# A third of unit 3's columns on ScalarE's DMA queue, and ScalarE's share of the normalisation in units 2 and 3

## The chip, the cores and the metric

The kernel runs on one core of one Trainium2 chip. Such a core has TensorE (PE), VectorE (DVE), ScalarE (ACT) and GpSimd (POOL), a sequencer SyncE (SP) that here only issues transfers, and 16 DMA engines between HBM and the on-chip memory (SBUF, 128 partitions). The metric is the device time of one execution in microseconds (us); the median of several runs counts, and one further execution was recorded by the hardware profiler.

## The reference

The input x has the shape (4, 8, 16, 256, 256) in float32: 512 channels of 65,536 elements, 134.2 MB. Each channel is normalised by its own mean and variance and multiplied by the channel's gamma:

```python
mu = x.mean(axis=(3, 4), keepdims=True)
var = ((x - mu) ** 2).mean(axis=(3, 4), keepdims=True)
x_norm = (x - mu) / np.sqrt(var + 1e-5)
out = x_norm * gamma[None, :, :, None, None]
```

The output is as large as the input, so 268.5 MB have to cross between HBM and SBUF.

## The kernel before

**Units.** The 512 channels are cut into 22 units, numbered from 0. The first and the last hold 16 channels, the 20 between them hold 24 (line 34). A unit is stored as 128 partitions of 2 or 3 columns, where a "column" is F = 4096 elements, 16 KB per partition. So a unit of two is 4 MiB (4.19 MB), a unit of three 6 MiB (6.29 MB), and each partition's part lies in one piece in HBM. A unit of three spreads each channel over partition thirds, so its column j has its own scale and shift on each partition. Four slots of SBUF (line 56) hold the units in turn; unit u lives in slot u % 4, is normalised in place and stored from there.

**Loads.** `load(u)` (lines 61 to 66) issues one DMA on SP's queue for a unit. Where `split` has an entry for the unit, its first column or columns go on ACT's queue instead, by a DMA of their own (line 64), and SP's DMA (line 66) takes the rest. Before the change only unit 1 is split, one column of three. The loads of units 0 to 3 are issued at once at the start; the load of unit u + 4 stands in the program behind the store of unit u (line 239) and waits on SP until that store has landed, since it takes the same slot.

**One unit's work** (lines 156 to 239). DVE sums the columns (line 161, or 165 for the units of two) while ACT squares them with an accumulated sum, column by column (line 168). TensorE adds the sums over the partitions of each channel (line 179 or 183), DVE forms the negative variance (187), ACT takes the root (191), DVE the reciprocal and the product with gamma (197, 204). In the units of three, TensorE spreads the two coefficients back to the partitions, into the tile `wide` (208). Then the columns are normalised: DVE takes them one by one (line 221), three of them, or two if the unit is in `helped`; in that case two small DVE instructions (214, 215) prepare the tile `own`, and ACT normalises the third column (216). In a unit of two that is helped, ACT takes 3/8 of the columns (229) and DVE the rest (233). The unit's store is issued by ACT, on ACT's queue (237).

**What sets the order.** Every engine works through its own instructions in the order of the program, unit after unit; semaphores hold it back where it needs another engine's result or a transfer. SP's queue therefore carries nothing but loads in the order of the units, and ACT's queue carries unit 1's first column and then the stores in the order of the units. Both queues are served by the same 16 DMA engines: a DMA over 128 partitions gives each engine 8 rows (one row is the piece of one partition: 16, 32 or 48 KB) and a short write to the semaphore at the end.

The lines that the change touches are these two:

```python
    split = {1: 1}

    helped = (0, 1)
```

Of the kernel before, what the change touches and what calls it, by code (L numbers as in the profile page):

```python
# [15 lines left out]
def kernel(  # L16
# [19 lines left out]
    starts = [sum(sizes[:i]) for i in range(U)]  # L36
    assert 8 * sum(sizes) == n_ch

    split = {1: 1}

    helped = (0, 1)

    xf = x.rearrange("b g c h w -> (b g c h w)")
    of = out.rearrange("b g c h w -> (b g c h w)")
# [225 lines left out]
```

## Time and profile before

| what | value |
|---|---|
| median of three runs | 627.42 us (627.4, 627.42, 630.28) |
| the profiled execution, its own time | 626.98 us |
| its span, from the first to the last instruction | 625.1 us |
| DVE busy | 438.4 us (70%) |
| ACT busy | 251.5 us (40%) |
| PE busy | 39.1 us (6%) |
| DMA | 268.50 MB, mean 430 GB/s over the span |
| share of the DMA engines' time | 50.4% for ACT's queue (q10), 49.1% for SP's (q1) |

The busy times are sums over the span; an engine that is busy for 70% isn't the limit for that reason alone. The share of the DMA engines' time by queue adds up to 99.5%, and that is the number to keep in mind. The profile's page cuts the span into 40 slices of 15.6 us and gives for each the busy share of every engine in tenths and the rate of the DMA in GB/s. Further views used below are the chain of work that ended last (in order of time), the list of who waited for whom, the instructions of one line with the times of their DMAs from issue to landing, the timeline of one engine, and stretches of time with the busy time of each engine and the DMA rate. "Landing" is the moment when the semaphore of a DMA is complete.

### The profile page before, as it was taken

The page shows a single profiled execution, that of the slowest core. Times are in us where ns is not written, and L with a number is a line of the kernel's source. Part 1 is how long each engine was busy: PE and PEld are TensorE (multiplying, and loading weights), DVE is VectorE, ACT ScalarE, POOL GpSimd, SP SyncE. Part 2 cuts the span into 40 slices and gives each one's busy share as a digit, 9 for nine tenths or more (in the row PEclk, how much of TensorE's full clock was granted, in tenths as well). Part 3 has the DMA queues.
Part 4 walks back from the last instruction along what each step waited for, and adds up shares of the span by engine and source line. Part 5 has one row for each costly group of instructions (what it writes and reads, how often), then busy time and mean ns, then how long its engine had stood idle before and what let it go on. Part 6 is the DMA issues. An engine that isn't in the chain of part 4 may idle for free.

```text
span 625.1 us, 1082 instructions
## 1 busy us (share of the span) xinstructions
PE 39.1 (6%) x280; PEld 36.6 (6%) x280; DVE 438.4 (70%) x179; ACT 251.5 (40%) x150; POOL 4.4 (1%) x17
## 2 busy tenths in 40 slices
PE   1000110101010100101010101010010101010100
PEld 1000110101010100101010101010010101010100
DVE  0789886858667585868686866758586868686780
ACT  0678253342607070615334261707062533426130
POOL 2000000000000000000000000000000000000000
DMA  9999999999999999999999999999999999999997
GB/s 384 438 400 437 437 450 406 453 431 425 450 413 440 440 421 443 434 428 443 415 447 440 418 447 428 434 440 418 443 440 421 443 425 435 443 421 426 440 441 338
DMA packets 6549, 268.50 MB, mean 430 GB/s; under 512 B 768, under 2 KB 784, under 8 KB 784
## 3 DMA queue, kind: packets, MB, share of 16 engines
q10 hardware_dynamic: 3312, 136.32, 50.4%
q1 hardware_dynamic: 3168, 132.12, 49.1%
q8 instruction: 2, 0.03, 0.0%
q14 instruction: 3, 0.02, 0.0%
q0 software_dynamic: 64, 0.01, 0.0%
HBM read 134.22 MB, written 134.23 MB: 429 GB/s over the span
## 4 chain that ended last, share of the span: by engine, by line
DMA 72%; DVE 22%; PE 1%; issue 1%; ACT 0%; SPq 0%; ACTq 0%
DMA xt<-in_x_dram 51%; DMA out_dram<-xt 22%; DVE st L161 15%; DVE xt L221 3%; DVE st L165 3%; DVE xt L233 1%; PE wide L208 1%; ACT std L191 0%; PE ps L179 0%; DVE nvar L187 0%; DVE rstd L197 0%; DVE coef L204 0%; PE ps L183 0%; DVE own L214 0%; DVE own L215 0%
## 5 line engine op out<-in xcount | busy, mean ns | idle before, releaser
L168 ACT ACTIVATE junk<-xt 128x4096 uint8<-128x4096 f32 (+1 forms) x62 | 231.0, 3727 | 290.7 <-DMA xt<-in_x_dram 278.4
L161 DVE TENSOR_REDUCE st<-xt 128x3 f32<-128x12288 f32 x20 | 259.1, 12953 | 99.5 <-DMA xt<-in_x_dram 99.5
L221 DVE TENSOR_SCALAR xt<-xt,wide 128x4096 f32<-128x4096 f32 x59 | 139.5, 2421 | 30.2 <-PE wide L208 30.2
L179 PE MATMUL ps<-st,navg 128*24 128x2 f32 x120 | 7.4, 178 | 498.7 <-DVE st L161 498.7
L179 PEld LDWEIGHTS ps<-st,navg 128*24 128x24 f32 x120 | 6.3, 126 | 499.8 <-issue 499.8
L208 PE MATMUL wide<-coef,spread 24*128 24x2 f32 x120 | 28.2, 347 | 23.0 <-DVE coef L204 23.0
L191 ACT ACTIVATE std<-nvar,eps_t 24x1 f32<-24x1 f32 (+1 forms) x22 | 6.5, 294 | 56.1 <-DVE nvar L187 56.1
L208 PEld LDWEIGHTS wide<-coef,spread 24*128 24x128 f32 x120 | 27.0, 321 | 24.1 <-issue 23.0
L165 DVE TENSOR_REDUCE st<-xt 128x1 f32<-128x8192 f32 x2 | 17.4, 8686 | 3.4 <-DMA xt<-in_x_dram 3.4
L187 DVE TENSOR_SCALAR nvar<-ps 24x1 f32<-24x1 f32 (+1 forms) x22 | 6.1, 276 | 12.6 <-PE ps L179 11.1
L168 ACT ACTIVATION_READ_ACCUMULATOR junk<-xt 128x1 f32 x62 | 11.6, 186 | 0.0
L119 DVE COPY g_two<-g_row 1x128 f32<-1x128 f32 x1 | 0.2, 214 | 11.3 <-DMA g_row<-in_gamma_dram 11.3
L197 DVE RECIPROCAL rstd<-std 24x1 f32<-24x1 f32 (+1 forms) x22 | 3.3, 152 | 6.7 <-ACT std L191 6.7
L233 DVE TENSOR_SCALAR xt<-xt,ps,coef 128x5120 f32<-128x5120 f32 (+1 forms) x2 | 7.5, 3748 | 0.0
L216 ACT ACTIVATE xt<-xt,own 128x4096 f32<-128x4096 f32 x1 | 3.8, 3803 | 2.4 <-DVE own L215 2.4
L204 DVE TENSOR_TENSOR coef<-rstd,g_col 24x1 f32<-24x1 f32 (+1 forms) x22 | 3.3, 148 | 0.8
L229 ACT ACTIVATE xt<-xt,shift,coef 128x3072 f32<-128x3072 f32 x1 | 2.9, 2947 | 0.7 <-DVE shift L228 0.7
L183 PE MATMUL ps<-st,navg 128*128 128x2 f32 x4 | 1.1, 349 | 28.4 <-DVE st L165 28.4
L196 DVE COPY coef<-ps 24x1 f32<-24x1 f32 x20 | 2.7, 135 | 0.0
L183 PEld LDWEIGHTS ps<-st,navg 128*128 128x128 f32 x4 | 1.0, 311 | 28.5 <-issue 28.5
L129 PE MATMUL g_ps<-one,g_rep 1*128 1x1 f32 x4 | 1.0, 345 | 13.0 <-DVE g_rep L126 13.0
L115 ACT ACT_TABLE_LOAD x1 | 1.3, 1283 | 1.2 <-PEq L254 1.2
(29 smaller groups left out, 10.2 us busy)
## 6 DMA issues: line engine op xcount, KB each, us to landing
out_dram<-xt ACTq DMA_DIRECT2D x20, 6144.0 KB, 49.2
xt<-in_x_dram SPq DMA_DIRECT2D x19, 6144.0 KB, 43.6
xt<-in_x_dram SPq DMA_DIRECT2D x3, 4096.0 KB, 26.3
out_dram<-xt ACTq DMA_DIRECT2D x2, 4096.0 KB, 22.1
xt<-in_x_dram ACTq DMA_DIRECT2D x1, 2048.0 KB, 17.2
out_dram<-touch POOLq DMA_DIRECT2D x1, 8.0 KB, 7.4
g_row<-in_gamma_dram POOLq DMA_DIRECT2D x1, 0.5 KB, 10.4
```

Source lines behind the costliest of these rows:

```text
L161: nc.vector.reduce_sum(out=st[:, u, :, 0], in_=t.rearrange("p (j f) -> p j f", j=3), axis=AX.X,)
L165: nc.vector.reduce_sum(out=st[:, u, 0, 0:1], in_=t, axis=AX.X)
L168: square = nc.scalar.activation(out=junk[:, :step], in_=t[:, j * step : (j + 1) * step], func=ACTF.Square, accum_out=st[:, u, j, 1:2],)
L179: nc.tensor.matmul(out=ps[:n], lhsT=navg3[:, j], rhs=st[:, u, j], start=j == 0, stop=j == 2,)
L187: nc.vector.tensor_scalar(out=nvar[:n, u : u + 1], in0=ps[:n, 0:1], scalar1=ps[:n, 0:1], scalar2=ps[:n, 1:2], op0=ALU.mult, op1=ALU.add,)
L191: nc.scalar.activation(out=std[:n, u : u + 1], in_=nvar[:n, u : u + 1], func=ACTF.Sqrt, bias=eps_t[:n], scale=-1.0,)
L197: nc.vector.reciprocal(out=rstd[:n, u : u + 1], in_=std[:n, u : u + 1])
L204: nc.vector.tensor_mul(out=coef[:n, u, 1:2], in0=rstd[:n, u : u + 1], in1=gamma_u)
L208: nc.tensor.matmul(out=wide[:, j], lhsT=spread[:, j], rhs=coef[:n, u], start=True, stop=True,)
L216: nc.scalar.activation(out=t[:, 2 * F :], in_=t[:, 2 * F :], func=ACTF.Identity, bias=own[:, 0:1], scale=own[:, 1:2],)
L221: nc.vector.tensor_scalar(out=t[:, j * F : (j + 1) * F], in0=t[:, j * F : (j + 1) * F], scalar1=wide[:, j, 0:1], scalar2=wide[:, j, 1:2], ...
L233: nc.vector.tensor_scalar(out=t[:, :cut], in0=t[:, :cut], scalar1=ps[:, 0:1], scalar2=coef[:, u, 1:2], op0=ALU.add, op1=ALU.mult,)
```

## The change

```diff
-    split = {1: 1}
-
-    helped = (0, 1)
+    split = {1: 1, 3: 1}
+
+    helped = (0, 1, 2, 3)
```

The first column of unit 3 (2.10 MB) is now loaded by a second DMA on ACT's queue, issued right behind that of unit 1 and ahead of every store; SP's DMA for unit 3 shrinks from three columns to two. In units 2 and 3 DVE normalises two columns instead of three, ACT normalises the third, and DVE runs the two small instructions for `own`. No byte more or less is moved. The order of the instructions is otherwise the same: ACT gets one DMA and two activations of 128x4096 more, DVE two tensor_scalar instructions of 128x4096 fewer and four small ones more.

## The prediction

> **What bounds the kernel now.** I read the 40 slices first, then the shares of the queues.
>
> ```profile
> span 625.1 us, 1082 instructions
> DMA  9999999999999999999999999999999999999997
> GB/s 384 438 400 437 437 450 406 453 431 425 450 413 440 440 421 443 434 428 443 415 447 440 418 447 428 434 440 418 443 440 421 443 425 435 443 421 426 440 441 338
> q10 hardware_dynamic: 3312, 136.32, 50.4%
> q1 hardware_dynamic: 3168, 132.12, 49.1%
> ```
>
> The DMA engines are busy in every slice, 99.5% over the span. The rates jitter because a transfer is counted in the slice where it starts; long stretches don't jitter, whichever queues are at work:
>
> ```profile
> 4.00:18.00 14.00, 2.35 (x36) 2.27 (x36) 1.02 (x7) 0.13 (x1) 1.74 (x5) 1.00 1.01 434
> 31.00:38.00 7.00, 0.00 (x0) 0.00 (x0) 7.00 (x2) 6.54 (x4) 0.00 (x0) 1.00 1.03 405
> 216.00:448.00 232.00, 14.23 (x96) 13.32 (x96) 165.44 (x64) 91.37 (x56) 0.00 (x0) 1.00 1.00 434
> ```
>
> The last column is GB/s: 434 for pure loads at the start, 434 for loads beside stores. 268.5 MB at 434 GB/s are 618.7 us of 625.1. The rest is the start (first data at 1.8 us), the end, and a dip at 31 to 38 us. So a change can gain almost nothing unless it moves fewer bytes, and this one moves the same. It can lose where the DMA engines run out of work. The place to look is the end, in the chain:
>
> ```profile
> 554.02 38.63 DMA xt<-in_x_dram
> 592.65 0.02 issue
> 592.67 8.70 DVE st L165
> ...
> 603.15 4.55 DVE xt L233
> ```
>
> and the waits and the stores' landing times:
>
> ```profile
> DVE st L161 <- DMA xt<-in_x_dram: 99.5, 17, 6.4
> SPq L66 <- DMA out_dram<-xt: 529.4, 18, 41.7
> DMA to landing us min/median/max: 16.3/49.2/49.8
> ```
>
> DVE waits for loads in 17 units, and SP waits for stores. The last load lands at 592.65; 15.1 us later (607.73) the last store is issued, and it lands 16.3 us after that (the minimum in the third row), at 624.05. It is 4.19 MB, 9.7 us at 434 GB/s. The fixed cost of a DMA on idle engines is read from the start: units 0 and 1a (I call unit 1's first column 1a and the rest 1b, likewise 3a and 3b), 6.29 MB, are issued at 0.81 and unit 0 lands 17.04 us later (the chain), 14.5 of them data: 2.5 us. So the last store could have landed 12.2 us after its issue; for the other 4.1 us it stood behind unit 20's store. **The last load has 4.1 us of slack; beyond that, each us that it comes later lengthens the kernel by one.**
>
> **How the queues share.** Two numbers fix it. 0 on SP's queue (32 KB rows) and 1a on ACT's (16 KB rows) land together, 17.0 and 17.2 us after their issue, and have 4 and 2 MiB: the queues take turns row by row, so shares go by row size. In steady state both have 48 KB rows and a load of 6.29 MB takes 29.0 us (ACT's first squares of units 19 and 20 start at 539.53 and 568.52), 217 GB/s, half. The last load, 32 KB rows beside 48 KB ones, takes 592.67 - 568.52 = 24.1 us: 174 GB/s, 0.4 of 434. Row by row fits all three.
>
> The Trainium skill, page "DMA: Bandwidth & Descriptors", section "Queues, rings and completion order", states that an engine round-robins between queues but drains a whole packet, typically 9 to 17 descriptors, before it switches. With the 9 of each DMA here, unit 0 would have landed about 5 us ahead of 1a; the trace has 0.2 us, so the rows speak against it. I keep it as a rival.
>
> **The change part by part.**
>
> *The DMA of 3a.* One more issue on ACT at about 1.2 us, 0.4 us long like the present one; ACT then has nothing to do until unit 0 lands at 17.87. Cost nothing. SP's issue for unit 3 stays, smaller. On ACT's queue 3a stands ahead of store 0.
>
> *18 to 32.5 us.* Up to 18 nothing changes. Then 1b had all of the bandwidth and landed at 27.5 (1.23 + 26.3). Now 1b (32 KB rows) shares 2:1 with 3a (16 KB): 6.29 MB, 14.5 us, both end at about 32.4. DVE reached unit 1 at 31.27, after normalising unit 0, so unit 1 starts 1.1 us later, and store 1 is issued at 53.6 instead of 52.44.
>
> *32.5 to 58 us.* Store 0 is issued at 31.58 as before. Its first row moved only at 36.5, by the trace's record of single transfers, which also shows that the rows under way then took 2.5 us instead of 1.8: that is the 405 GB/s above, some 0.7 us lost. Now ACT's queue was active until 32.4, and store 0 should begin at about 34 to 35. It took 23.1 us from first row to landing (59.57), so it lands at 57.8, 1.8 earlier. Unit 2 shares with it 0.6 to 0.4 from 34 on instead of running alone from 27.5: it lands at about 55.5 instead of 47.6. DVE had started unit 2 at 52.27, so it now waits 3 us for it.
>
> *58 to 83 us.* Store 1 ran beside unit 3's 48 KB rows at half rate, 29.0 us. 3b has 32 KB rows, so store 1 gets 0.6, 6.29 MB at 260 GB/s = 24.2 us, a little more once 3b is through: it lands at about 82.6 instead of 88.53, **5.9 earlier**. 3b lands at about 79 instead of 74.1.
>
> *Steady state.* From here both queues halve the bandwidth as before. The bytes moved up to any time are the same, but for at most 0.28 MB from the 0.7 us saved, so stores 5.9 us early mean loads 4.6 to 5.9 us late: I take 5.3. A load is issued when the store four units earlier lands, and had 14.5 us of lead (unit 20's row: 554.02 issue of unit 21, 568.52 its turn); that grows. Stores had lead too: issued 562.73 (unit 19), in turn at 579.6; it shrinks by about 11 us to some 6, against 2.4 at least that store 0 needed from issue to first row. No queue runs dry, so the lag stays.
>
> *The end.* The last load lands at 598.0, the last store is issued at 613.0 and lands at 613.0 + 2.5 + 9.7 = 625.2 instead of 624.05: **+1.2 us**.
>
> The Trainium skill, same page, section "Anatomy of one DMA", puts the fixed cost of a DMA at about 2.0 us; by that the loss would be 0.7. The trace's 2.5 us decides.
>
> *The help in units 2 and 3.* Each saves one of three DVE passes (7.09 to 4.75 us, the rows of units 2 and 1 at line 221) and adds two small ones (0.3 us): 2.0 us, and ACT adds 3.80 us beside DVE. Stores 2 and 3 are issued 2.0 us earlier than they otherwise would be (about 76.7 for store 2), but ACT's queue is with store 1 until 82: covered. Without that cover it would be a gain of 2.0 us per unit, at the start only. Worth: nothing. ACT's own next work, unit 3's and 4's squares, waits for loads anyway (it waited 14 us for unit 4).
>
> *Unknown: how soon a store starts when ACT's queue is nearly empty.* Nothing before shows this at the end. Nearest rows: 2.5 us fixed at the start, and store 0's 4.9 us from issue to first row (5.3 with the landing) in the middle of busy loads. I take 2.5, as the engines are idle then; the other end gives +4.0. Below, with a lag of 4.6 and 1.9 us, the slack covers all: 0.
>
> Sum: span 625.1 + 1.2 = 626.3, plus 1.9 us around it (626.98 - 625.1) = 628.2 for the profiled execution; the median of the runs stands 0.4 above it: **628.6 us**. No change (within 0.5%, 3.1 us, about what a measurement of this kernel can tell), with a slight loss.
>
> **Rivals.**
>
> *No lag, 627.4.* If ACT's queue runs dry after store 0 (store 1 is ready at 53.6 + 2.4 to 4.9, needed at 57.8), loads catch up; a lag below 4.1 us costs nothing. For it: the margin is under 2 us. With the saved restart, 626.7 at best. The page's rule of whole packets also ends here: store 1's turn would end at 80.8 with or without 3a on ACT's queue, unit 4 at 95.3 in both, lag 0, 627.4; the landings of 0 and 1a speak against it. 20%, 3% of it by that rule.
>
> *Slower, 633.* The last load comes 7 us late and the last store needs 5.3 us plus data: 607.73 + 7 + 5.3 + 9.7 = 629.7, +5.7, 633.1. It would take store 0 right behind 3a at 32.5, with no gap, 4 us earlier. It decides over 0.5% from a sum of lag and start cost over 9.7 us (here 7.8). Against it: store 0 can't have a row before 34. 13%.
>
> *Faster by over 0.5%* needs 3.1 us that DMA engines busy for 99.5% don't have; 3% for what I don't see.
>
> **How the numbers follow.** Forecast 64%, its own range 627.6 to 630.4. The range takes in the first rival and half of the second: 626.7 to 631.2. Faster 0.03, same 0.64 + 0.20 = 0.84, slower 0.13.
>
> **What would show it.** Rate 434 in all long stretches; DVE waiting for units 1, 2 and 3 (17 waits become 19 or 20); 1b landing near 32.4; SP's load of unit 5 issued near 82.6 instead of 88.60; DVE's reduction of unit 4 at about 108.5 instead of 103.38, of unit 21 at 598 instead of 592.67; the last store's landing time near 12.2 instead of 16.3, with a gap in DMA before it. Wrong would be: a load lag under 4 us (no loss) or over 6, idle DMA in mid-kernel, or a rate other than 434 with 16 KB rows.

## The result: slower by 1%, and the profile after

Over ten executions each, the changed kernel takes 635.41 us in the median (630.61 to 637.53) and the kernel before 627.41 us (626.74 to 632.33): a ratio of 1.0102, with a 95% interval of 1.007 to 1.0133. The profiled execution of the changed kernel took 635.56 us, 8.58 us more than the 626.98 us of before. The forecast was 628.6, its range ended at 631.2, and a loss of over 0.5% had a chance of 0.13.

The page of the changed kernel, its 40 slices and the shares of the queues:

```profile
span 633.7 us, 1096 instructions
...
DMA  9999999999999999999999999999999999999997
GB/s 381 435 408 421 423 425 425 437 414 425 428 429 431 413 444 437 422 434 441 422 425 434 425 416 431 431 428 441 434 431 425 425 434 410 432 434 434 430 406 324
DMA packets 6693, 268.50 MB, mean 424 GB/s; under 512 B 784, under 2 KB 800, under 8 KB 800
...
q10 hardware_dynamic: 3456, 138.41, 50.7%
q1 hardware_dynamic: 3168, 130.02, 48.5%
```

The same bytes, and DMA engines that are still busy for 99.2% of the span, but of a longer span. The loss is therefore no idle time: rows take longer. A long stretch in mid-kernel (from, to, length, busy time of PE, PE loads, DVE, ACT and POOL, clock, DMA share, GB/s) says so too:

```profile
216.00:448.00 232.00, 13.09 (x88) 12.21 (x87) 164.21 (x60) 91.09 (x55) 0.00 (x0) 1.00 1.00 430
```

Before it was 434 at the same share of 1.00. The chain of work that ended last (start, length, what), first the beginning of the kernel, then its end:

```profile
32.61 12.96 DVE st L161
...
56.65 12.97 DVE st L161
...
80.53 12.96 DVE st L161
...
110.42 12.96 DVE st L161
...
557.17 49.36 DMA xt<-in_x_dram
606.55 8.70 DVE st L165
...
617.02 4.55 DVE xt L233
```

and the waits and the stores' times from issue to landing:

```profile
SPq L66 <- DMA out_dram<-xt: 532.5, 18, 42.0
...
DVE st L161 <- DMA xt<-in_x_dram: 117.2, 20, 8.8
```

```profile
L237 ACTq DMA_DIRECT2D out_dram<-xt x22: 338/338/351, 31.6 to 621.6; - x22
...
DMA to landing us min/median/max: 11.1/39.4/44.2
```

The first four lines of the chain are units 1 to 4, and they start 0.2 to 1.9 us later than the forecast had them (32.4, 55.5, 79 and 108.5). Then it goes astray: the last load lands at 606.53, **13.9 us** later than before, where 5.3 were forecast. The last store is issued at 621.60 and lands 11.1 us later, at 632.69; before it took 16.3. So the end absorbs 5.2 of the 13.9 us, and 8.7 are left. The lag had two parts: unit 4's load was 7.0 us late already (110.42 against 103.38), and from there to the last load it grew by another 6.9.

The trace's record of single transfers shows what the 13.9 us are. At a landing, each of the 16 DMA engines reports by itself. The last load was reported done between 590.86 and 592.65 before (mean 591.48), and between 599.36 and **606.53** after (mean 602.79). DVE waits for the last of the 16. So the engines are late by 11.3 us in the mean, and the slowest is late by another 2.6 because they no longer run in step. A row of 48 KB takes 1.81 us on its engine, 27.08 KB per us; summed over each engine's rows, the time beyond that rate (called **stretch** below) is 1.76 us per engine before and 8.64 us after, 7.26 of it in load rows.

### The profile page after: what moved, and what is told of

Same layout as the page of the kernel before. It is cut to its first block, busy times and chain, and to the rows that moved or that the text cites. A ratio compares the mean times of both kernels' runs of the same rounds, so it can differ in the third digit from the quotient of the medians.

```text
span 633.7 us, 1096 instructions
## 1 busy us (share of the span) xinstructions
PE 39.1 (6%) x280; PEld 36.6 (6%) x280; DVE 434.4 (69%) x181; ACT 259.1 (41%) x152; POOL 4.4 (1%) x17
## 4 chain that ended last, share of the span: by engine, by line
DVE 57%; DMA 19%; another core or an unknown queue 15%; PE 5%; issue 1%; ACT 1%; SPq 0%; DVEq 0%
DVE st L161 35%; DVE xt L221 18%; DMA xt<-in_x_dram 13%; DMA out_dram<-xt 6%; PE wide L208 4%; DVE st L165 1%; PE ps L179 1%; ACT std L191 1%; DVE nvar L187 1%; DVE xt L233 1%; DVE rstd L197 0%; DVE coef L204 0%; PE ps L183 0%; DVE own L214 0%
## 5 line engine op out<-in xcount | busy, mean ns | idle before, releaser
L221 DVE TENSOR_SCALAR xt<-xt,wide 128x4096 f32<-128x4096 f32 x57 | 134.7, 2418 | 27.1 <-PE wide L208 27.1
L187 DVE TENSOR_SCALAR nvar<-ps 24x1 f32<-24x1 f32 (+1 forms) x22 | 6.1, 276 | 12.6 <-PE ps L179 11.1
L216 ACT ACTIVATE xt<-xt,own 128x4096 f32<-128x4096 f32 x3 | 11.4, 3802 | 7.1 <-DVE own L215 7.1
(29 smaller groups left out, 11.3 us busy)
```

Of the source, the lines that this page charges most:

```text
L187: nc.vector.tensor_scalar(out=nvar[:n, u : u + 1], in0=ps[:n, 0:1], scalar1=ps[:n, 0:1], scalar2=ps[:n, 1:2], op0=ALU.mult, op1=ALU.add,)
L216: nc.scalar.activation(out=t[:, 2 * F :], in_=t[:, 2 * F :], func=ACTF.Identity, bias=own[:, 0:1], scale=own[:, 1:2],)
L221: nc.vector.tensor_scalar(out=t[:, j * F : (j + 1) * F], in0=t[:, j * F : (j + 1) * F], scalar1=wide[:, j, 0:1], scalar2=wide[:, j, 1:2], ...
```

## The experiments

The recorded expectations name theories by letters. A: the two queues change from one DMA to the next at another distance from each other (their phase). B: ACT's help in units 2 and 3 disturbs the DMA. C: the 16 KB rows of 3a, or the DMA more, cost by themselves. D: the DMA engines fall into two groups that take store 0 in different turns. E: stores are issued too shortly before their turn. F: a store 0 that comes early hurts, a later one heals. Medians are over all executions of a kernel, ratios are against the kernel before beside it; single executions of before range from 626.7 to 634.5 over all comparisons, so a difference of under 1 us between two medians says nothing.

### Each half of the change alone

```diff
 # split only                      # help only
     split = {1: 1, 3: 1}              split = {1: 1}
     helped = (0, 1)                   helped = (0, 1, 2, 3)
```

> Unit 3's first column on ScalarE's queue, the normalisation shared in units 0 and 1 only. Theory A (the shifted phase of the two queues: loads some 5 us later, stores some 6 us earlier against each other, costs slow rows in mid-kernel and makes the 16 DMA engines drift apart): as the changed kernel, about 634 to 636, the last load landing after 603, its spread over the engines above 5 us. Theory B (ScalarE's normalisation of units 2 and 3 disturbs the DMA): 627 to 628.5, the last load near 598.

> Only the normalisation of units 2 and 3 is shared; unit 3 is loaded whole on SyncE's queue. Theory A: as the kernel before, 627 to 628, last load near 592.7. Theory B: 632 to 636.

The split alone takes 635.05 us, ratio 1.008 (1.0048 to 1.0112); the help alone 628.43 us, ratio 0.999 (0.9965 to 1.0015). The whole loss belongs to 3a on ACT's queue, and B falls. (The profiled execution of the split alone was its fastest, 630.66; it shows the same in small: last load between 594.8 and 601.4, a spread of 6.5 us, stretch 3.0 per engine.)

### Other ways to move the phase

```diff
 # after, with the store of unit 2 in three DMAs
+        if u == 2:
+            nc.scalar.dma_start(out=rows(of, u)[:64, :F], in_=t[:64, :F])
+            nc.scalar.dma_start(out=rows(of, u)[:64, F:], in_=t[:64, F:])
+            nc.scalar.dma_start(out=rows(of, u)[64:], in_=t[64:])
 # before, with the load of unit 4 in three DMAs
+        if u == 4:
+            nc.sync.dma_start(out=home(u)[:64, :F], in_=rows(xf, u)[:64, :F])
+            nc.sync.dma_start(out=home(u)[:64, F:], in_=rows(xf, u)[:64, F:])
+            nc.sync.dma_start(out=home(u)[64:], in_=rows(xf, u)[64:])
```

> The changed kernel, but the store of unit 2 goes in three DMAs on ScalarE's queue: 64 partitions whole, and the other 64 in rows of 16 and 32 KB. That is 12 turns on each engine instead of 8, so loads gain about 2 rows of 3.6 us, 7 us, on stores, and the phase is back near that of the kernel before; the column of unit 3 on ScalarE's queue stays. Theory A: 626.5 to 629, DMA rows in mid-kernel unstretched. Theory C (the 16 KB rows or the additional load on ScalarE's queue do the harm, for instance because the engines fall out of step at 34 us, whatever the phase): 633 to 636.

> The kernel before, but the load of unit 4 goes in three DMAs on SyncE's queue, 64 partitions whole and 64 in rows of 16 and 32 KB: 12 turns instead of 8, so loads fall about 7 us behind and stores come about 7 us earlier. Nothing else is changed. Theory A: the loss comes without unit 3's column on the other queue, 632 to 638 with slow rows and drift; of it about 3 us from the end alone (lag of 7 us against 4.1 us of slack). Theory C: no slow rows in mid-kernel, only the end's 3 us, 629.5 to 631.

With the cut store: 634.65 us, ratio 1.0095 (1.0065 to 1.0124). By its number it is what theory C had forecast (633 to 636), not A (626.5 to 629). But the cut threw the engines out of step itself: from unit 3's store on, landed at 159.87, the 16 reports of a store are some 11.6 us apart. So it decides nothing. With the cut load: 710.39 us, ratio 1.1318 (1.1253 to 1.1384), beyond every theory's number. Its page:

```profile
DMA  9999999999999999999999999989898999997476
GB/s 384 432 408 452 381 367 306 428 429 417 401 396 401 401 412 406 412 395 389 373 389 373 389 370 367 375 362 412 348 395 370 389 389 381 399 382 321 178 331 285
```

The rate falls from 70 to 124 us (the fifth to seventh slice, of 17.7 us each), where the three pieces run. It returns to 428 for two slices and then stays below that to the end, though every later DMA is as before: stretch 45.7 us per engine, and the reports of one load end up to 46 us apart. As a test of the phase it failed, but it shows how much engines that are out of step can cost.

### Moving store 0 by less than one microsecond

When store 0 is issued in the changed kernel, at 31.62 us, the load rows are just turning over: 3a and 1b end at 31.6 to 32.1, and a load row of unit 2 begins. The trace's rows on three of the 16 engines (the trace doesn't number the engines, the numbers here are for reference; each row is put behind the one that ended just before it. S1 is the DMA of 3a, L1 that of 1b, S2 store 0, L2 unit 2, after the dot the row, counted from 0, where 8 is the short write to the semaphore, after @ its start, in brackets its stretch, in underscores idle time):

```
engine 1:  S1.7@31.0 L1.8@31.6 S1.8@31.6 L2.0@31.6 L2.1@33.4(+0.57) S2.0@35.8 L2.2@37.0(+0.58) S2.1@39.4
engine 4:  S1.7@31.0 L1.8@31.6 S1.8@31.6 L2.0@31.6 L2.1@33.4 _0.90_ L2.2@36.2(+0.26) S2.0@38.2 L2.3@39.5
engine 14: S1.7@31.2 L1.8@31.8 S1.8@31.8 L2.0@31.8 L2.1@33.6 L2.2@35.5(+0.87) S2.0@38.1 L2.3@39.3
```

Seven engines took store 0 after load row 1 (first rows at 35.7 to 36.2 us), nine after row 2 (38.1 to 38.4). In the kernel before all 16 took it in the same turn, at 36.5 to 36.9. From here on the queues alternate, so that the order of this moment stays. Hence the next runs: the changed kernel with store 0 a little later, by an activation on ACT that copies 640 elements of unit 0 onto themselves ahead of it; and the kernel before with 400 elements, meant to split its engines into groups.

```diff
+        if u == 0:
+            nc.scalar.activation(out=t[:, cut : cut + 640], in_=t[:, cut : cut + 640], func=ACTF.Identity)
         nc.scalar.dma_start(out=rows(of, u), in_=t)
```

> The changed kernel with store 0 issued some 0.95 us later: ScalarE copies 640 elements of unit 0 in place first. In the changed kernel store 0's first row came after the load row of about 33.5 us on 7 DMA engines and after the next one on the other 9, so the engines stood in two groups from then on. With the delay all 16 should take it after the same row. Theory D (the two groups are what makes the engines drift apart and the last load land late on the slowest): 628 to 630.5, spread of the last load's landing over the engines below 3 us. Theory A (the phase of the queues does it): 633 to 636 as the changed kernel.

> The kernel before with store 0 issued some 0.75 us later (400 elements copied in place), so that its first row should fall on both sides of the load rows that start from 33.95 to 34.45 us: two groups of engines, without unit 3's column on the other queue. Theory D: 631 to 636, spread of the last load above 5 us. Theory A: 627 to 628.5 as the kernel before.

The changed kernel with this delay takes **627.38 us**, ratio 0.9984 (0.9957 to 1.0011): all of the loss is gone, with 3a on ACT's queue and ACT's help as they were. The lines of the added activation and of the stores, and the chain's end:

```profile
L238 ACT ACTIVATE xt<-xt x1: 736/736/736, 31.7 to 31.7; 128x640 f32<-128x640 f32 x1
```

```profile
L239 ACTq DMA_DIRECT2D out_dram<-xt x22: 338/338/353, 32.4 to 611.4; - x22
...
DMA to landing us min/median/max: 12.7/42.0/44.6
```

```profile
508.34 42.00 DMA out_dram<-xt
...
550.39 45.91 DMA xt<-in_x_dram
596.30 0.02 issue
596.32 8.70 DVE st L165
```

Store 0 is issued at 32.44 instead of 31.62, all 16 engines take it at 37.7 to 38.1, stretch is 1.77 us per engine and the last load's spread 1.77, as before. The last load lands 3.65 us later than before, within the slack of the end, and the span is 625.1 us, as before. So C falls too: 16 KB rows and one DMA more cost nothing that can be measured. The time is below both forecasts, D's (628 to 630.5) and A's (633 to 636, which counted on an unchanged phase). Unit 4's load, 7.0 us late in the changed kernel, is 3.4 late here:

```profile
106.82 12.96 DVE L161 TENSOR_REDUCE st<-xt 128x3 f32<-128x12288 f32 x1 [7.79 <-DMA xt<-in_x_dram]
```

and from there to the last load the lag grows by 0.2 us, not by 6.9.

The kernel before with its delay: 627.89 us, ratio 0.9987 (0.9959 to 1.0015). Nine of ten executions took 627.3 to 628.4; the profiled one took 633.67, with the engines in groups of ten and six, a spread of 9.9 us and stretch 4.3. Six engines took store 0 one turn before the other ten, and six reports of the last load came at 595.5 to 599.3, the other ten at 589.4 to 591.2.

### Earlier stores throughout

```diff
+        some = 1 if 4 <= u <= 20 else 3
             nc.vector.reduce_sum(
-                out=st[:, u, :, 0], in_=t.rearrange("p (j f) -> p j f", j=3), axis=AX.X,
+                out=st[:, u, :some, 0],
+                in_=t[:, : some * F].rearrange("p (j f) -> p j f", j=some), axis=AX.X,
             ...
-        for j in range(cols // step):
+        for j in range(some if three else cols // step):
```

> The changed kernel, but the statistics of units 4 to 20 are taken from the first column alone (two thirds of the sums and squares are left out), so their stores are issued some 8.6 us sooner after the load has landed and wait 16 us instead of 8 in ScalarE's queue. Units 0 to 3 and the last unit are untouched, so the phase and the groups are those of the changed kernel. Theory E (the stores' lead has become so short that queues restart and rows are stretched): 628.5 to 631. Theories A and D: 633 to 636.

Sums and squares of units 4 to 20 cover one column of three here (`st` is set to zero once at the start, not shown), so their stores are issued 8.5 us sooner after the load's landing. Still 633.76 us, ratio 1.0072 (1.0038 to 1.0107), with a spread of 7.1 us and stretch 6.4. Short notice for the stores isn't the cause: E falls.

### Two groups, or the distance between the queues?

Further delays of store 0, with 1930, 2130, 2290 and 2950 elements in the changed kernel and 800 in the kernel before, were to separate D from F.

> The changed kernel with store 0 issued some 1.9 us later (1930 elements copied in place), a whole load row of 1.8 us more than the changed kernel's own issue, so its first row should again fall on both sides of a row boundary. Theory D (two groups of engines): slow again, 632 to 636, spread of the last load's landing above 4 us, although 0.95 us less of delay was 627.4. Theory F (later is better: the store has only to come late enough): 627 to 628.5.

> The same with some 2.75 us (2950 elements), a row and a half: all engines should take the store after the same row. Theory D: 627 to 628.5, spread of the last load's landing near 1.8 us. Theory F: 627 to 628.5. A third possibility, that any delay beyond 1 us costs its own time: above 629.

> The kernel before with store 0 issued some 0.95 us later (800 elements), aimed at the middle of the load rows' starts (33.95 to 34.45 us). One of the ten executions with 0.6 us of delay had two groups of engines and took 633.67. Theory D: most executions with two groups, median 630 to 635, without unit 3's column on the other queue. Theory A (a loss only with that column): 627 to 628.5.

> The changed kernel with store 0 some 2.1 us later (2130 elements): with 1930 elements 15 engines took the store after one load row and a single one after the next, so that run missed its aim by about 0.2 us. Here the split should be more even. Theory D (two groups of engines in the shifted phase make the loss, however late the store): 630 to 636, spread of the last load's landing above 4 us. Theory F (a later store 0 heals the change, whatever the groups): 627 to 628.5.

> The same with some 2.2 us (2290 elements), the next step up. Theory D: 630 to 636 if both groups have several engines, 627 to 628.5 if all but one or two engines have moved on to the later row. Theory F: 627 to 628.5 in both cases.

They took 627.64 (ratio 0.9981, 0.9959 to 1.0004), 627.38 (0.9982, 0.9957 to 1.0008), 628.99 (0.9999, 0.9975 to 1.0024), 627.55 (0.9978, 0.9955 to 1.0002) and 628.45 us (1.0005, 0.9978 to 1.0031). The first of them missed its aim of two equal groups (15 engines to 1), but the before kernel with 800 elements and the changed one with 2290 hit it, 8 to 8: and they lose nothing that can be measured. So it isn't two groups as such. The last runs ask the opposite: store 0 earlier, so that all 16 engines take it in the early turn, with no groups. It leaves 1220 and 840 elements per partition of unit 0 unnormalised. Beside it the changed kernel again, and one with a delay of 160 elements.

```diff
-                    out=t[:, cut:], in_=t[:, cut:], func=ACTF.Identity,
+                    out=t[:, cut : cols - 840], in_=t[:, cut : cols - 840], func=ACTF.Identity,
+            less = 1220 if u == 0 else 0
-                out=t[:, :cut], in0=t[:, :cut], scalar1=ps[:, 0:1],
+                out=t[:, : cut - less], in0=t[:, : cut - less], scalar1=ps[:, 0:1],
```

> The changed kernel with store 0 issued some 0.7 us earlier: 1220 columns of VectorE's part and 840 of ScalarE's part of unit 0 are left unnormalised. All engines should take store 0 after the load row that starts at 33.4 to 33.9 us, as 7 of the 16 did in the changed kernel. Theory D (the changed kernel loses since its store 0 falls on a row boundary and splits the engines): 627 to 629, spread of the last load's landing below 3 us, though the store comes earlier. Theory F (an early store 0 is what hurts, a later one heals): 633 to 637.

> The changed kernel once more, for a second profile of it: 633 to 637 by all theories. Theory D: two or more groups of engines at store 0, with several engines in each, and a spread of the last load's landing above 5 us.

> The changed kernel with store 0 some 0.4 us later (160 elements copied), between the changed kernel and the run with 0.82 us, which was at 627.4. Theory D: most engines already take the later row; 628 to 633, executions of both kinds. Theory F: between the two as well, without groups.

Early: **634.68 us**, ratio 1.0077 (1.0048 to 1.0106). All 16 engines took store 0 in the same turn (36.0 to 36.6), and yet it is as slow as the changed kernel: D falls as the cause of the loss, F holds. Its stores' line and the chain's end:

```profile
L238 ACTq DMA_DIRECT2D out_dram<-xt x22: 338/338/353, 30.9 to 619.2; - x22
...
DMA to landing us min/median/max: 11.1/38.7/42.2
```

```profile
579.89 12.97 DVE st L161
...
604.15 8.70 DVE st L165
```

The changed kernel again: 632.76 us, ratio 1.006 (1.0032 to 1.0088), with single executions from 628.09 to 634.96; in its profile nine engines took store 0 one turn before the other seven, the spread is 7.3 us and stretch 7.1. The 160 elements: 631.04 us, ratio 1.0044 (1.0018 to 1.0071), halfway.

### What the runs have in common

What differs between the good and the bad ones is read from two lines each of the timelines of DVE and SP. Unit 5's load landed when DVE starts its reduction, and unit 3's store landed when SP issues the next load. The kernel before, the changed, the delayed (640) and the early one, in this order:

```profile
132.95 12.95 DVE L161 TENSOR_REDUCE st<-xt 128x3 f32<-128x12288 f32 x1 [6.41 <-DMA xt<-in_x_dram]
147.28 0.33 SPq L66 DMA_DIRECT2D xt<-in_x_dram  x1
```

```profile
140.12 12.95 DVE L161 TENSOR_REDUCE st<-xt 128x3 f32<-128x12288 f32 x1 [6.54 <-DMA xt<-in_x_dram]
145.98 0.33 SPq L66 DMA_DIRECT2D xt<-in_x_dram  x1
```

```profile
136.68 12.95 DVE L161 TENSOR_REDUCE st<-xt 128x3 f32<-128x12288 f32 x1 [6.70 <-DMA xt<-in_x_dram]
143.81 0.33 SPq L66 DMA_DIRECT2D xt<-in_x_dram  x1
```

```profile
139.97 12.95 DVE L161 TENSOR_REDUCE st<-xt 128x3 f32<-128x12288 f32 x1 [5.84 <-DMA xt<-in_x_dram]
143.90 0.33 SPq L66 DMA_DIRECT2D xt<-in_x_dram  x1
```

A store lands 14.3 us after a load in the first, 5.9 in the second, 7.1 in the third and 3.9 in the fourth. A turn of one load row and one store row takes 3.63 us, so these are about four, between one and two, two, and one turns. The table counts on each engine the load rows that start between the end of a load and the last row of the store that ends next, and gives the profiled execution's stretch per engine. Where rows of several engines start within nanoseconds of each other, the stitching is ambiguous, so the counts and the stretch of single groups are rough in the changed kernel and in the one with short sums; their means over 16 engines, 8.6 and 6.4 us, don't depend on it:

```
kernel                    engines: rows between   stretch of these, us   median, us (ratio)
before                    16: 3                   1.8                    627.41
help only                 16: 3                   2.2                    628.43 (0.9990)
before, 800 elements      8: 3, 8: 4              3.6, 3.8               628.99 (0.9999)
changed, 2950 elements    16: 2                   2.4                    627.38 (0.9982)
changed, 2290 elements    8: 1, 8: 2              3.3, 3.6               628.45 (1.0005)
changed, 2130 elements    13: 1, 3: 2             1.9, 3.1               627.55 (0.9978)
changed, 1930 elements    15: 1, 1: 2             2.0, 2.2               627.64 (0.9981)
changed, 640 elements     16: 1                   1.8                    627.38 (0.9984)
changed, 160 elements     16: 1                   2.4                    631.04 (1.0044)
changed                   6: 0, 8: 1, 2 vary      9.9, 7.6, 9.0          635.41 (1.0102)
changed, short sums       11: 0, 5: 1             7.1, 4.9               633.76 (1.0072)
changed, store 0 early    16: 0                   6.0                    634.68 (1.0077)
```

**Where the load queue and the store queue change to their next DMA with no load row between them, on all or on some of the engines, load rows are stretched and the engines drift apart; with one to four rows between, the medians show no loss, but for the delay of 160 elements.** That the moment of store 0's issue decides is shown by moving it both ways, by less than a microsecond. That the rows between are how it acts is read from the table; no run moves them in another way. Why a change of both queues in the same turn stretches rows, and why in the changed kernel engines with one row between suffer along with the others, isn't shown.

In the profile of the split alone (630.66) they don't suffer. Four engines took store 0 at 35.6 to 35.8 us, the other twelve at 37.9 to 38.4. Four of the 16 reports of unit 2's load come 1.5 to 2.0 us behind the first; at unit 7 four come 5.2 to 5.6 behind, at the last load 5.8 to 6.5, at 600.6 to 601.4. The other twelve come at 594.8 to 597.2, much as in the delayed kernel (594.5 to 596.3). So four engines alone make that load late. That they are the four that took store 0 first fits, but the trace can't prove it.

Two things stay open. The delay of 160 elements has one row between on all 16 engines in its profile, and still ran 0.4% over before. In that execution store 0 was issued at 32.41, practically as with 640 elements (32.44), since unit 0's work had begun later; unit 3's store landed 7.3 us after unit 5's load, again as there (7.1). So in single executions neither the issue nor the rows between settle the time: this one (630.88) has a single engine with some 7 us of stretch, on which the last load lands at 600.22 while the other 15 are done by 597.4. The help alone (630.71) has such a single late engine in its profile too, and the 2950 elements (630.79) have two; these are kernels whose medians are as before. And the one execution of 633.67 of the kernel before with 400 elements has no engine with fewer than three rows between. What sets off these was not found.

## Why the prediction was wrong

- **What bounds the kernel** was right: DMA engines busy all through, loads that DVE waits for (20 times now, as forecast), and a last load whose lateness counts beyond the slack.
- **Row by row turns, and the steps up to 110 us** were right in order: 1b landed at 32.51 (32.4 forecast), unit 2 at 56.62 (55.5), 3b at 80.44 (79), SP's load of unit 5 was issued at 85.40 (82.6), unit 4 landed at 110.40 (108.5). The errors are 0.1 to 2.8 us, less than one turn. But store 0 began later than forecast, at 35.7 to 38.4 instead of 34 to 35, and landed at 59.90, 0.3 us later than before and not 1.8 earlier (57.8); store 1 came 3.2 us earlier than before, not 5.9. The Trainium skill's rule that an engine drains a packet of typically 9 to 17 descriptors before it turns to the next queue (page "DMA: Bandwidth & Descriptors", section "Queues, rings and completion order") isn't borne out: in the rows above L2 and S2 alternate singly.
- **The help is worth nothing**: right, 0.999 (0.9965 to 1.0015). The DVE time saved went into waits for loads: 106.8 us with the help alone, 99.5 before.
- **The slack at the end**: the logic was right, since 13.9 less 5.2 is the loss of 8.7. Its size was off: the fixed cost of the last store was 11.1 - 9.7 = 1.4 us, not the 2.5 read from the start (and outside the 1.9 to 5.3 that the prediction allowed), so the slack is 5.2 and not 4.1. In the undisturbed delayed kernel the last load is 3.65 us late and nothing is lost, which fits either size.
- **The step that failed is "Steady state": "No queue runs dry, so the lag stays".** The lag didn't stay: it was 7.0 us at unit 4, where 5.1 were forecast, and 13.9 at the last load instead of 5.3. The lag of the shift alone was overestimated: in the delayed kernel, the nearest thing to it, it was 3.65 us. By itself it would have cost nothing, and the time would have been the 627.4 of the first rival. What came on top is a term that the sum didn't have. Steady state was priced at 434 GB/s as before, with 16 engines acting as one. In fact, beyond the delayed kernel's 3.6, the loads came another 7.7 us late in the mean over the engines (6.9 of it is the growth of stretch), and the slowest engine another 2.6 by drifting apart: 3.6 + 7.7 + 2.6 = 13.9. That this comes with store 0's issue is shown by the delayed and the early kernel; why rows stretch stays open. The text named "a rate other than 434 with 16 KB rows" among what would make it wrong. It did fall, to 430, but not through 16 KB rows.
- **The rival "Slower, 633"** came near by luck, and by its number only. Its price was a last load 7 us late and a last store with 5.3 us beyond its data; they were 13.9 and 1.4. Its condition, a store 0 right behind 3a at 32.5, didn't come about: store 0's first rows came at 35.7 to 38.4. The reason against it ("store 0 can't have a row before 34") was true; the loss came another way.
- **The missed rival** could have been named from the prediction's own rows: store 0 issued at 31.58 and 1b and 3a ending at about 32.4 (it became 31.62, and 31.6 to 32.1) say that engines may decide differently, and all 16 have to report before anybody goes on. Its price couldn't have been read there: nothing in the profile of before shows a stretch of 8 us.

## What to carry to other kernels

In this kernel, with two DMA queues that share the engines at full rate, the moment at which the first store starts fixed an order that 600 us didn't undo. In a kernel of this kind, look at the landings of both queues, and try what happens with more rows between them. When a kernel is a per cent slower with busy DMA engines and the same bytes, compare the reports of one DMA's 16 engines (590.9 to 592.7 against 599.4 to 606.5 here) before looking for work that was added. Move a suspect by less than a row's time, both ways: 0.8 us later gave 627.4, 0.7 us earlier 634.7. Take more than one profile of each kernel, since single executions of the same kernel differ by as much as the effect (628.1 to 637.5 for the changed kernel). None of the versions was measurably faster than the kernel before, so the change brings nothing even where it does no harm.

## What the runs showed of the hardware that was not expected

- One DMA cut once into three of 64 partitions, in a load queue that is otherwise the same, costs 13% of the whole kernel (710.39 against 627.4 us): its effect lasts from 124 us to the end at 707.
- Beside a busy load queue, store 0 didn't take the next turn. In the three runs where all engines took it in a common turn and the times are given here, its first row came 4.9 to 5.7 us after the issue: issue at 30.91, first rows at 36.0 to 36.6; at 31.58 (before), 36.5 to 36.9; at 32.44, 37.7 to 38.1.
- The load rows beside store 0's start are stretched: by up to 1.0 us in the changed kernel (rows that start at 33.4 to 37.5), by 0.5 to 0.8 us in the kernel before (34.0 to 34.4). In the slow kernels that goes on at later changes: in the early one an engine loses 3.9 us between 100 and 580 us, and 3.3 of them between 5 and 11 us after a load's landing, shortly after a store has landed and the next has begun.
- The last store, on engines that had just run out of other work, took 1.4 us beyond its data from issue to landing (first row 0.85 us after its issue), the first loads 2.5.
